# One step of a hybrid attention layer: keys and queries stored in DRAM with both parts of a row side by side, and output weights scaled while they are rounded

## The chip, the cores and the metric

The kernel runs on one NeuronCore of a Trainium2 chip. The metric is the device time of one launch in microseconds (us), the median of several runs; lower is better. TensorE (PE) does the matmuls and transposes, VectorE (DVE), ScalarE (ACT) and GpSimd (POOL) the rest, and nearly all DMAs are issued by SyncE (SP), in order, on one queue.

## The reference

One layer is run for a prompt of 2048 tokens and for a sample of 64 tokens that has a cache of 512 earlier ones. All is float32; the model width is 1024.

```python
h = rmsnorm(x, g_pre)
fq, fk, fv, ff, fg, dq, dk, dv, dg = split(h @ w_in)    # eight groups of 512 columns, ff of 8
# fox: 8 heads of 64; cum = cumulative sum of log_sigmoid(ff + b_f)
s = fq . fk / 8 + cum[query] - cum[key];  causal;       fox_o  = softmax(s) @ fv
# diff: 4 heads with two query/key halves of 64 and values of 128
s1, s2 = q1 . k1 / 8 + bias, q2 . k2 / 8 + bias;        # T5 bias, mask by chunks of 64
diff_o = rmsnorm((softmax(s1) - lam * softmax(s2)) @ dv, subln_g) * 0.8
out = concat(fox_o * silu(fg), diff_o * silu(dg)) @ w_out
y = x + rmsnorm(out, g_post)                            # also returned: k, v, log-forget rows
```

## The kernel before

**Two parts of a value.** Matmuls run on float32r operands. A value x is kept as h, its rounding to float32r, and l, the exact rest; a product takes three matmuls (h by h, h by l, l by h). Rounding is a copy on ScalarE that writes h, and a subtraction on VectorE or GpSimd that writes l.

**Stages.** The prompt is cut into four blocks of 512 tokens; the sample joins block 0. `Proj.block` multiplies a block with the eight groups of 512 weight columns. Keys (`k_out`), values (`v_out`), gates (`g_out`) and queries (`qgroup`) go to scratch tensors in DRAM, from which `Attn` loads them. The attention of a block goes on beside the projection of the next; the output projection (`Out`) goes on beside the attention of the last block. There are eight units, four pairs of fox heads and four diff heads; a unit has two "heads" `hd` in the scores (two fox heads, or the two halves of a diff head).

**The order.** Every piece of work is a function with a place on one line that is measured in TensorE time; the pieces are emitted in the order of their places, and a planner sets semaphores and the order of each engine's queue. The loads of the attention run ahead in rings: `Ring` issues the next load when a slot is freed. `caps = (4, 4, 6, 2, 2)` are the slots for keys, values, queries, biases and gates.

**Keys.** A score needs q.k with h and l parts. A head's keys are an operand of 128 rows: the 64 rows of the h part and the 64 rows of the l part, so that one matmul of 128 rows by the queries (h over l) gives hh + ll, and a second by the queries (l over h) gives the mixed products. In DRAM there is a tensor `KS[b]` per block of [2 heads, 8 units, 128 rows, 512 keys]. `k_out` turns a tile of 128 tokens over on TensorE, splits it into h and l in a slot `khl`, and stores it with two DMAs, one per head (L968). `want_k` loads an operand tile of up to 1024 keys with a DMA per block (L194).

**Queries.** `QD[b]` is [2, 8, 128, 512] (576 for block 0, with the sample). `qgroup` scales a piece (512 tokens; in block 0 two pieces of 288) into `qf`, rounds it into one half of a slot `qhl` (L1015), writes the rest into the other half (L1017), and stores it with one DMA per head (L1019). The slots `qhl`, `khl` and `vhl` share a tag with two buffers, so a slot must be stored before the next but one piece is rounded. `want_q` makes two tiles for 256 queries of a head: the (h over l) one with one DMA (L267), and the (l over h) one with two DMAs of 64 rows each (L270).

**Running sums.** `CUM[b]` holds [8, 512] per block; `want_cum` loads up to 1024 of them, repeated over all partitions, with a DMA per block (L285).

**Output weights.** `Out.weights` loads w_out in 16 pieces of 128 by 512 for k = 0 to 7, rounds each on ScalarE (L1200) and lets GpSimd compute the rest (L1201). For the diff heads, k = 4 to 7, ScalarE scales the piece in place first (L1199). Its place is the end of the last projection. The output projection uses k in the order 4, 5, 6, 7, 0, 1, 2, 3 (L1274 to L1276; L1269 and L1270 for the sample).

Of the kernel before, what the change touches and what calls it, by code (L numbers as in the profile page):

```python
# [9 lines left out]
F32 = mybir.dt.float32  # L10
# [7 lines left out]
P = 128  # L18
# [15 lines left out]
# T5 bucket of rel = key - query over the runs of rel in which it is constant  # L34
# (NUM_BUCKETS = 32, MAX_DISTANCE = 128, bidirectional); every rel below -90 is bucket 15.
# [10 lines left out]
class Ring:  # L46
    """Loads that run ahead of their use, as many as there are free slots."""
# [43 lines left out]
def hybrid_step(ctx: ExitStack, tc: tile.TileContext, ins, outs):  # L91
# [43 lines left out]
    QD = [dr.tile([2, 8, P, BLK + (DEC if b == 0 else 0)], F32, name=f"QD{b}") for b in range(NBLK)]  # L135
# [4 lines left out]
    CUM = [dr.tile([8, BLK], F32, name=f"CUM{b}") for b in range(NBLK)]  # L140
# [5 lines left out]
    def rsqrt_newton(pool, v, out, rows, n, tag, eng=None):  # L146
        """out = 1/sqrt(v): exp(-ln(v)/2) and one Newton step."""
# [11 lines left out]
    # ------------------------------------------------------------------ attention  # L159
    class Attn:  # L160
        """Attention of one range of query tiles, over every unit (two fox heads or one diff head)."""
# [9 lines left out]
        def asked(self):  # L171
            """A thunk that queues the loads asked for since the last call."""
# [9 lines left out]
        # ---- loads  # L182
        @staticmethod
        def key_edges(nk):
            """The keys of every tile of them: two blocks, or one at the front."""
            at = list(range(nk % (2 * BLK), nk, 2 * BLK))
            return list(zip([0] + at, at + [nk])) if at[:1] != [0] else list(zip(at, at[1:] + [nk]))

        def want_k(self, got, u, hd, nk):
            def load(k0, k1):  # L190
                def go():
                    t = self.p["k"].tile([P, 2 * BLK], F32R, name="kg", tag="k")
                    for c in range(k0, k1, BLK):
                        nc.sync.dma_start(out=r32(t[:, c - k0:c - k0 + BLK]), in_=KS[c // BLK][hd, u])  # L194
# [5 lines left out]
        def want_kc(self, got, u):  # L200
            """The sample's keys of a unit: both heads' operands, the cached ones and the new ones."""
# [13 lines left out]
            def second():  # L215
# [5 lines left out]
                # the order of the parts doesn't matter  # L221
# [38 lines left out]
        def want_q(self, got, u, hd, col, w):  # L260
            def load(s):
                def go():
                    t = self.p["q"].tile([P, 256], F32R, name="qg", tag="q")
                    src = QD[0] if col >= SEQ else QD[col // BLK]
                    c0 = BLK if col >= SEQ else col % BLK
                    if s == 0:
                        nc.sync.dma_start(out=r32(t[:, :w]), in_=src[hd, u, :, c0:c0 + w])  # L267
                    else:
                        for a in (0, 64):
                            nc.sync.dma_start(out=r32(t[a:a + 64, :w]), in_=src[hd, u, 64 - a:P - a, c0:c0 + w])  # L270
                    got.append(t)
                return go
            for s in (0, 1):
                self.want(self.Q, load(s))

        def want_cum(self, got, h, nk, sample):
            def load(c0, w):
                def go():
# [3 lines left out]
                    else:  # L282
                        for a in range(c0, c0 + w, BLK):
                            ww = min(BLK, c0 + w - a)
                            nc.sync.dma_start(out=t[:, a - c0:a - c0 + ww],  # L285
                                              in_=bcast_row(CUM[a // BLK][h, 0:ww], ww))
# [5 lines left out]
        def want_strip(self, got, h, nk, sample):  # L292
            """The bias of the last columns up to the diagonal; before them it is that of bucket 15."""
# [46 lines left out]
            # chunks of at most a bank, none narrow where that can be avoided  # L340
# [46 lines left out]
        def store_mix(self, mix, u, pair, w):  # L387
            """mix: f32 [128 mix columns, w tokens], in SBUF."""
            nc.sync.dma_start(out=(MN if pair is None else MS[pair])[u], in_=mix[:, :w])

        # ---- sub-jobs: (A thunks, B thunks, thunks of the step after)
        def fox(self, u, hd, pair, ctxu, first, last, sample=False):
            """One head, one pair of query tiles (or the sample's tile)."""
# [7 lines left out]
            for j, t in enumerate(tiles):  # L401
# [14 lines left out]
                if j == len(tiles) - 1:  # L416
                    def endA():
                        self.Q.free(); self.Q.free()
# [1084 lines left out]
```

## Time and profile before

| What | Value |
|---|---|
| Runs | 1841.08, 1832.17 and 1841.0 us; median 1841.0 |
| Span of the profiled execution, first to last instruction | 1837.8 us; the page gives no time around it |
| Busy: PE, DVE, ACT, POOL | 1736.8, 1189.6, 1128.9, 768.2 us |
| Mean granted TensorE clock | 0.982 |
| DMA | 308170 packets, 361.38 MB, 197 GB/s over the span |

Lines of the profile name a line of the kernel (L351), the engine, the operation, and the tiles as output<-inputs with shapes. A group shows its count, busy time, the mean in ns of one, then the engine's idle time just before its instructions and what ended that idle time. A row of waits reads: who waited, for whom, us in total, number of times, the longest. A row of windows holds the stretch, its length, busy time and number of instructions of PE, PE's weight loads, DVE, ACT and POOL, then the granted clock (1.00 is full), the busy share of the DMA engines, and GB/s. A row of a source line shows a queue's instruction with count, the shortest, median and longest time of its issue in ns, and the first and last start. A row of DMA issues ends with KB per DMA and the median us from issue to landing.

### The profile page before, as it was taken

Reading aid. Unit: us, or ns where it says so; the run is one execution under the profiler, and the core shown is the slowest. Engines: PE = TensorE matmul, PEld = TensorE weight load, DVE = VectorE, ACT = ScalarE, POOL = GpSimd, SP = SyncE. Lnnn points to the kernel's source line nnn. Section 1 sums busy time; section 2 is a strip of 40 time slices with the busy share of each in tenths; the row PEclk is TensorE's granted clock in tenths of the full one; section 3 lists DMA queues with packets and bytes.
Section 4 is the critical chain, followed back from the end, with each engine's and each line's share of the span. In section 5 each row is a group of like instructions: output and inputs, shape, how many; then the busy total and the mean of one; then the engine's idle time right before and its main releaser. Section 6 shows DMA issues by size and latency. Waiting matters only on the chain. (4 is left out here: it accounts for less than half of the span.)

```text
span 1837.8 us, 31858 instructions
## 1 busy us (share of the span) xinstructions
PE 1736.8 (95%) x9828; PEld 1467.4 (80%) x9828; DVE 1189.6 (65%) x3274; ACT 1128.9 (61%) x2518; POOL 768.2 (42%) x1083
## 2 busy tenths in 40 slices
PE   7888999999999999989999999999989999999998
PEld 5676888777877778878888888888878878887887
DVE  5422555556668576656776678878867876666764
ACT  4533656465767666665666657667776666556663
POOL 2204235345354453343323225555795663322331
PEclk9998999999999999999999999999989999999999
DMA  7787579789868766867777667667665464455433
GB/s 203 240 193 193 162 217 273 205 245 233 218 209 246 213 196 195 233 170 230 219 229 224 177 181 216 195 195 224 199 219 166 145 189 156 153 181 156 145 115 108
DMA packets 308170, 361.38 MB, mean 197 GB/s; under 512 B 41808, under 2 KB 202732, under 8 KB 308000
## 3 DMA queue, kind: packets, MB, share of 16 engines
q1 hardware_dynamic: 306384, 356.93, 66.9%
q0 software_dynamic: 672, 2.38, 0.4%
q8 instruction: 79, 1.29, 0.3%
q14 instruction: 91, 0.75, 0.1%
q10 hardware_dynamic: 944, 0.03, 0.0%
HBM read 263.89 MB, written 97.70 MB: 197 GB/s over the span
## 5 line engine op out<-in xcount | busy, mean ns | idle before, releaser
L372 ACT ACTIVATE prob<-prob,mn 128x1024 f32<-128x1024 f32 (+8 forms) x400 | 356.1, 892 | 180.7 <-DVE mn L359 179.5
L351 PE MATMUL S<-kg,qg 128*128 128x512 f32 (+4 forms) x1344 | 375.8, 373 | 20.5 <-DVE mn L359 10.0
L497 DVE TENSOR_TENSOR ptl<-pt,pth 128x512 fp32r<-128x512 f32 (+3 forms) x456 | 284.4, 636 | 94.8 <-ACT pth L496 92.3
L868 PE MATMUL acc<-wh,xx 128*128 128x512 f32 x752 | 303.4, 408 | 18.9 <-ACT wh L776 14.9
L869 PE MATMUL acc<-wl,xx 128*128 128x512 f32 x752 | 300.6, 401 | 8.5 <-DVE wl L777 8.5
L870 PE MATMUL acc<-wh,xx 128*128 128x512 f32 x752 | 300.6, 400 | 0.1
L496 ACT CAST pth<-pt 128x512 fp32r<-128x512 f32 (+3 forms) x456 | 237.6, 545 | 81.9 <-PE pt L490 65.4
L351 PEld LDWEIGHTS S<-kg,qg 128*128 128x128 f32 (+1 forms) x1344 | 226.6, 188 | 62.0 <-DVE mn L359 18.8
L490 PE MATMUL pt<-ident,prob 128*128 128x128 f32 (+2 forms) x1692 | 257.6, 274 | 4.7 <-ACT pts L637 2.2
L490 PEld LDWEIGHTS pt<-ident,prob 128*128 128x128 f32 (+2 forms) x1692 | 200.2, 142 | 26.6 <-ACT pts L637 3.3
L777 POOL TENSOR_TENSOR wl<-wraw,wh 128x512 fp32r<-128x512 f32 x126 | 167.4, 1345 | 121.2 <-ACT wh L776 91.0
L408 POOL TENSOR_TENSOR dg<-bias,cmask 128x128 f32<-128x128 f32 (+1 forms) x136 | 66.1, 486 | 281.8 <-DVE mn L359 188.4
L868 PEld LDWEIGHTS acc<-wh,xx 128*128 128x128 f32 x752 | 144.2, 193 | 49.7 <-ACT wh L776 17.2
L869 PEld LDWEIGHTS acc<-wl,xx 128*128 128x128 f32 x752 | 144.6, 192 | 37.3 <-DVE wl L777 11.5
L521 PE MATMUL av<-pth,vg 128*128 128x256 f32 (+1 forms) x576 | 158.3, 294 | 9.4 <-DVE oT L537 4.7
L870 PEld LDWEIGHTS acc<-wh,xx 128*128 128x128 f32 x752 | 144.0, 191 | 28.4 <-DVE xx L745 0.6
L521 PE MATMUL av<-ptl,vg 128*64 128x256 f32 (+1 forms) x576 | 140.3, 283 | 3.9 <-DVE ptl L497 3.6
L776 ACT CAST wh<-wraw 128x512 fp32r<-128x512 f32 x168 | 100.5, 618 | 69.1 <-DMA wraw<-in_w_in 59.9
L359 DVE CUSTOM_DVE_ANT_0 prob<-S,bias,mn 128x512 f32<-128x512 f32 (+4 forms) x200 | 115.3, 577 | 28.8 <-DMA bias<-CUM 14.5
L521 PE MATMUL avd<-pth,vg 128*128 128x256 f32 (+1 forms) x576 | 131.6, 288 | 2.3 <-ACT pth L496 2.3
L521 PEld LDWEIGHTS av<-pth,vg 128*128 128x128 f32 x576 | 110.0, 191 | 21.5 <-issue 7.7
L453 POOL TENSOR_SCALAR gate<-gate,rr 128x64 f32<-128x64 f32 (+1 forms) x136 | 61.5, 463 | 140.2 <-DMA gate<-GS 57.9
(257 smaller groups left out, 3611.8 us busy)
## 6 DMA issues: line engine op xcount, KB each, us to landing
wraw<-in_w_in SPq DMA_DIRECT2D x168, 256.0 KB, 4.8
vg<-VS SPq DMA_DIRECT2D x80, 512.0 KB, 4.1
kg<-KS SPq DMA_DIRECT2D x160, 256.0 KB, 4.1
bias<-CUM SPq DMA_DIRECT2D x80, 256.0 KB, 5.6
wst<-in_w_in SPq DMA_DIRECT2D x64, 256.0 KB, 5.6
out<-ef SPq DMA_DIRECT2D x64, 256.0 KB, 3.3
VS<-vhl SPq DMA_DIRECT2D x32, 512.0 KB, 4.6
KS<-khl SPq DMA_DIRECT2D x64, 256.0 KB, 4.7
```

The costliest lines, as they stand in the source:

```text
L351: nc.tensor.matmul(S[:rows, :c1 - c0], q()[s][:, qc:qc + rows], kg()[ki][:, c0 - k0:c1 - k0], start=(s == 0), stop=(s == 1))
L359: nc.vector.tensor_tensor_reduce(out=pr[:rows, a - p0:b - p0], in0=S[:rows, a - c0:b - c0], in1=ap()[:rows, a - b0:b - b0], scale=1.0, sca ...
L372: nc.scalar.activation(out=pr, in_=pr, func=AF.Exp, scale=-1.0, bias=st["m"][:rows, i - 1:i], accum_out=st["s"][:rows, h:h + 1])
L490: nc.tensor.transpose(pt[:rk, off:off + rows], self.key_tile(sts[j], rows, kt, rk), ident[:rows, :rows])
L496: nc.scalar.copy(h[:rk, :off], pt[:rk, :off])
L497: nc.vector.tensor_tensor(out=l[:rk, :off], in0=pt[:rk, :off], in1=r32(h[:rk, :off]), op=ALU.subtract)
L521: nc.tensor.matmul(st["av"][:vs.stop - vs.start, j0 * rows:W], ctxu["v"][kt // 4][:rk, kt % 4, vs], g["p"][part][:rk, o:o + w], start=(kt ...
L776: nc.scalar.copy(h, raw[:, :BLK])
L777: (nc.vector if many or k % 4 == 3 else nc.gpsimd).tensor_tensor(out=l, in0=raw[:, :BLK], in1=r32(h), op=ALU.subtract)
L868: nc.tensor.matmul(a, x[0][:, c0:c0 + rows], wh, start=s, stop=False)
L869: nc.tensor.matmul(a, x[0][:, c0:c0 + rows], wl, start=False, stop=False)
L870: nc.tensor.matmul(a, x[1][:, c0:c0 + rows], wh, start=False, stop=e)
```

## The change

Keys of the whole prompt lie in one tensor `KS` of [128 rows, 8 units, 2 parts, 2048]: rows 0 to 63 are head 0, 64 to 127 head 1, and the h and l parts of a row are next to each other in the third dimension. A tile of keys is stored with one DMA. An operand tile of up to 1024 keys is loaded with one DMA of 64 rows by 2 parts; its rows are then h, l, h, l in turn instead of all h and then all l. A row of queries is stored per pair of tiles as h, l, h (3 x 256), so that one load with overlapping reads makes both operands, (h, l) rows and (l, h) rows, side by side in one tile of 512 columns; this takes a second store of the h part. The ring of queries has 3 slots of twice the width instead of 6. Block 0's queries are cut in pieces of 256 and 256 + 64 tokens instead of 288 and 288, and the sample's 64 go to a tensor `QN` of their own. The running sums lie in one tensor. The output weights are taken in the order 4 to 7, 0 to 3; for the diff heads ScalarE scales and rounds in one instruction, and the rest is computed on VectorE with the scale in the same instruction. All comments are dropped as well.

```diff
-    KS = [dr.tile([2, 8, P, BLK], F32, name=f"KS{b}") for b in range(NBLK)]
+    KS = dr.tile([P, 8, 2, SEQ], F32, name="KS")
-    QD = [dr.tile([2, 8, P, BLK + (DEC if b == 0 else 0)], F32, name=f"QD{b}") for b in range(NBLK)]
+    QD = [dr.tile([8, P, 3 * BLK], F32, name=f"QD{b}") for b in range(NBLK)]
+    QN = dr.tile([8, P, 3 * DEC], F32, name="QN")
-    CUM = [dr.tile([8, BLK], F32, name=f"CUM{b}") for b in range(NBLK)]
+    CUM = dr.tile([8, SEQ], F32, name="CUM")
...
-                    for c in range(k0, k1, BLK):
-                        nc.sync.dma_start(out=r32(t[:, c - k0:c - k0 + BLK]), in_=KS[c // BLK][hd, u])
+                    nc.sync.dma_start(out=r32(t[:, :k1 - k0]), in_=KS[hd * 64:hd * 64 + 64, u, :, k0:k1])
...
+            def go():
+                t = self.p["q"].tile([P, 512], F32R, name="qg", tag="q")
+                rows = slice(hd * 64, hd * 64 + 64)
+                if col >= SEQ:
+                    for o in (0, 64):
+                        nc.sync.dma_start(out=r32(t[o:o + 64, :2 * w]), in_=QN[u, rows, o:o + 2 * w])
+                else:
+                    c0 = 3 * (col % BLK)
+                    a = QD[col // BLK][u, rows, c0:c0 + 2 * w]
+                    nc.sync.dma_start(out=r32(t[:, :2 * w]),
+                                      in_=bass.AP(a.tensor, a.offset, [a.ap[0], [w, 2], a.ap[1]]))
+                got.extend((t[:, :w], t[:, w:2 * w]))
+            self.want(self.Q, go)
...
-                        for a in range(c0, c0 + w, BLK):
-                            ww = min(BLK, c0 + w - a)
-                            nc.sync.dma_start(out=t[:, a - c0:a - c0 + ww],
-                                              in_=bcast_row(CUM[a // BLK][h, 0:ww], ww))
+                        nc.sync.dma_start(out=t[:, :w], in_=bcast_row(CUM[h, c0:c0 + w], w))
...
-            for i, a in enumerate((0, 64)):
-                nc.sync.dma_start(out=sc[i, u0:u0 + 4, :, r0:r0 + rows].rearrange("u (s r) t -> r (u s) t", s=2),
-                                  in_=r32(hl[a:a + 64, :, :rows]))
+            if t == 16:
+                ...
+            else:
+                nc.sync.dma_start(out=KS[:, u0:u0 + 4, :, t * P:(t + 1) * P].rearrange("r u s t -> r (u s) t"),
+                                  in_=r32(hl[:, :, :rows]))
...
+            pieces = [[(0, 2, 256)]] if nt <= BLK else [[(0, 1, 256)], [(256, 1, 256), (BLK, 1, DEC)]]
...
+                        for s0, n, m in segs:
+                            o = s0 - t0
+                            v = hl[:, 2 * o:2 * (o + n * m)].rearrange("p (a v t) -> p a v t", a=n, v=2)
+                            d = (QN[u0 + c] if s0 == BLK else
+                                 QD[b][u0 + c, :, 3 * s0:3 * (s0 + n * m)]).rearrange("p (a z) -> p a z", a=n)
+                            fs = f[:, o:o + n * m].rearrange("p (a t) -> p a t", a=n)
+                            nc.scalar.copy(v[:, :, 0], fs)
+                            nc.vector.tensor_tensor(out=v[:, :, 1], in0=fs, in1=r32(v[:, :, 0]), op=ALU.subtract)
+                            nc.sync.dma_start(out=d[:, :, 2 * m:], in_=r32(v[:, :, 0]))
+                            nc.sync.dma_start(out=d[:, :, :2 * m],
+                                              in_=r32(v).rearrange("p a v t -> p a (v t)"))
...
-            for k in range(KC):
+            for k in (4, 5, 6, 7, 0, 1, 2, 3):
...
                         if k >= 4:
-                            nc.scalar.activation(out=raw[:, :BLK], in_=raw[:, :BLK], func=AF.Copy, scale=subl)
-                        nc.scalar.copy(h[:, :BLK], raw[:, :BLK])
-                        nc.gpsimd.tensor_tensor(out=l[:, :BLK], in0=raw[:, :BLK], in1=r32(h[:, :BLK]),
-                                                op=ALU.subtract)
+                            nc.scalar.activation(out=h[:, :BLK], in_=raw[:, :BLK], func=AF.Copy, scale=subl)
+                            nc.vector.scalar_tensor_tensor(out=l[:, :BLK], in0=raw[:, :BLK], scalar=subl,
+                                                           in1=r32(h[:, :BLK]), op0=ALU.mult, op1=ALU.subtract)
+                        else:
+                            nc.scalar.copy(h[:, :BLK], raw[:, :BLK])
+                            nc.gpsimd.tensor_tensor(out=l[:, :BLK], in0=raw[:, :BLK], in1=r32(h[:, :BLK]),
+                                                    op=ALU.subtract)
...
-    caps = (4, 4, 6, 2, 2)
+    caps = (4, 4, 3, 2, 2)
```

More of the change, by code (lines that the diff above doesn't have):

```diff
@@ L260, in want_q @@
         def want_q(self, got, u, hd, col, w):
[L261 to L274, printed above, removed]
+            def go():
[11 more added lines that the diff above has]
+            self.want(self.Q, go)
         def want_cum(self, got, h, nk, sample):
@@ L417, in endA @@
                     def endA():
-                        self.Q.free(); self.Q.free()
+                        self.Q.free()
                         if last:
@@ L604, in endA @@
             def endA():
-                for _ in range(4):
+                for _ in range(2):
                     self.Q.free()
@@ L966, in k_out @@
             nc.vector.tensor_tensor(out=l, in0=x, in1=r32(h), op=ALU.subtract)
-            for i, a in enumerate((0, 64)):
-                nc.sync.dma_start(out=sc[i, u0:u0 + 4, :, r0:r0 + rows].rearrange("u (s r) t -> r (u s) t", s=2),
-                                  in_=r32(hl[a:a + 64, :, :rows]))
+            if t == 16:
+                for i, a in enumerate((0, 64)):
+                    nc.sync.dma_start(out=KN[i, u0:u0 + 4].rearrange("u (s r) t -> r (u s) t", s=2),
+                                      in_=r32(hl[a:a + 64, :, :rows]))
+            else:
+                nc.sync.dma_start(out=KS[:, u0:u0 + 4, :, t * P:(t + 1) * P].rearrange("r u s t -> r (u s) t"),
+                                  in_=r32(hl[:, :, :rows]))
         def g_out(self, g, t, f, rows):
@@ L986, in qgroup @@
             u0 = 0 if g == "fq" else 4
-            nb = 1 if nt <= BLK else 2
-            N = nt // nb
+            pieces = [[(0, 2, 256)]] if nt <= BLK else [[(0, 1, 256)], [(256, 1, 256), (BLK, 1, DEC)]]
             th = []
@@ L991, in qgroup, with step @@
                 e = {}
-                for i in range(nb):
-                    def step(k, c=c, i=i, e=e):
+                for i, segs in enumerate(pieces):
+                    t0 = segs[0][0]
+                    N = sum(n * m for _, n, m in segs)
+                    def step(k, c=c, i=i, e=e, t0=t0, N=N):
                         def go():
@@ L999, in go @@
                             o = e[i][:, :N]
-                            cs, xs_ = slice(c * P, (c + 1) * P), slice(i * N, (i + 1) * N)
+                            cs, xs_ = slice(c * P, (c + 1) * P), slice(t0, t0 + N)
                             nc.tensor.matmul(o, wh[:, cs], xh[:, xs_], start=(k == 0), stop=False)
@@ L1003, in go @@
                             nc.tensor.matmul(o, wl[:, cs], xh[:, xs_], start=False, stop=(k == KC - 1))
-                            if c == 3 and i == nb - 1 and freew:
+                            if c == 3 and i == len(pieces) - 1 and freew:
                                 self.W.free()
@@ L1007, in qgroup, with evac @@
                     th += [(3 * N / 2400.0, step(k)) for k in range(KC)]
-                    def evac(c=c, i=i, e=e):
+                    def evac(c=c, i=i, e=e, segs=segs, t0=t0, N=N):
                         f = self.p["e"].tile([P, BLK], F32, name="qf", tag="ef")
                         hl = self.p["e"].tile([P, 2 * BLK], F32R, name="qhl", tag="er", bufs=2)
-                        h, l = hl[:, :N], hl[:, N:2 * N]
-                        nc.vector.tensor_tensor(out=f[:, :N], in0=e[i][:, :N], in1=st["rbc"][:, i * N:(i + 1) * N],
+                        nc.vector.tensor_tensor(out=f[:, :N], in0=e[i][:, :N], in1=st["rbc"][:, t0:t0 + N],
                                                 op=ALU.mult)
-                        nc.scalar.copy(h[:, :N], f[:, :N])
-                        nc.vector.tensor_tensor(out=l[:, :N], in0=f[:, :N], in1=r32(h[:, :N]), op=ALU.subtract)
-                        for j, a in enumerate((0, 64)):
-                            nc.sync.dma_start(out=QD[b][j, u0 + c, :, i * N:(i + 1) * N].rearrange("(s r) t -> r s t", s=2),
-                                              in_=r32(hl[a:a + 64, :2 * N]).rearrange("r (s t) -> r s t", s=2))
+                        for s0, n, m in segs:
[9 more added lines that the diff above has]
+                                              in_=r32(v).rearrange("p a v t -> p a (v t)"))
                     th.append((0.5, evac))
@@ L1152, in sums @@
                 nc.vector.tensor_copy(cumlast, cum[:, BLK - 1:BLK])
-                nc.sync.dma_start(out=CUM[b], in_=cum)
+                nc.sync.dma_start(out=CUM[:, b * BLK:(b + 1) * BLK], in_=cum)
             def sample():
@@ L1181, in weights @@
         def weights(self):
-            self.w = []
+            self.w = {}
             th = []
-            for k in range(KC):
+            for k in (4, 5, 6, 7, 0, 1, 2, 3):
                 def go(k=k):
```

4 lines of the change are left out of this document (1 added, 3 removed).

## The prediction

> **What bounds the kernel now.** I read the page's first part, then TensorE's waits, then windows of the stages that the change touches, and last the issues of SyncE's queue.
>
> ```profile
> span 1837.8 us, 31858 instructions
> PE 1736.8 (95%) x9828; PEld 1467.4 (80%) x9828; DVE 1189.6 (65%) x3274; ACT 1128.9 (61%) x2518; POOL 768.2 (42%) x1083
> ```
> ```profile
> PE acc L868 <- ACT wh L776: 14.9, 7, 5.9
> PE S L351 <- DVE mn L359: 10.0, 13, 2.7
> PE acc L869 <- DVE wl L777: 8.5, 2, 5.0
> PE S L351 <- DMA qg<-QD: 5.8, 6, 2.5
> ```
> ```profile
> 300.00:900.00 600.00, 567.54 (x3156) 467.99 (x3155) 384.10 (x1103) 379.67 (x900) 258.37 (x403) 0.98 0.77 217
> 900.00:1300.00 400.00, 392.30 (x2308) 337.30 (x2307) 301.15 (x848) 269.33 (x591) 168.92 (x216) 1.00 0.70 203
> ```
>
> TensorE is busy for 1736.8 of 1837.8 us, so everything that is not TensorE can give at most 101 us, and that is split over many small waits: the longest group is 14.9 us. The change removes no matmul, so its gain can only come out of these waits and out of the time at a lower granted clock. From 300 to 900 us TensorE idles 600 - 567.5 = 32.5 us; from 900 to 1300 us it idles only 7.7 us. The two stretches differ in what their rows show beside it: the DMA engines are 0.77 against 0.70 busy.
>
> **The loads.** The rows of the queue, and the issues with their time to landing:
>
> ```profile
> L267 SPq DMA_DIRECT2D qg<-QD x144: 319/386/1775, 143.2 to 1735.8; - x144
> L270 SPq DMA_DIRECT2D qg<-QD x288: 444/522/1989, 144.9 to 1737.4; - x144
> L194 SPq DMA_DIRECT2D kg<-KS x160: 319/422/1775, 137.5 to 1717.4; - x160
> L285 SPq DMA_DIRECT2D bias<-CUM x80: 319/426/2224, 81.8 to 1750.4; - x80
> L968 SPq DMA_DIRECT2D KS<-khl x64: 580/627/1722, 109.6 to 1291.4; - x64
> L1019 SPq DMA_DIRECT2D QD<-qhl x80: 574/610/1852, 139.2 to 1217.1; - x80
> ...
> qg<-QD SPq DMA_DIRECT2D x128, 128.0 KB, 3.1
> qg<-QD SPq DMA_DIRECT2D x256, 64.0 KB, 4.0
> kg<-KS SPq DMA_DIRECT2D x160, 256.0 KB, 4.1
> KS<-khl SPq DMA_DIRECT2D x64, 256.0 KB, 4.7
> ```
>
> Queries: each of 128 operands (a pair of tiles, a head) needs one issue of 0.386 us and two of 0.522 us, 1.43 us. One load replaces them. Its source has three dimensions; its issue costs between 0.386 us (L267, two dimensions) and 0.610 us (L1019, three). I take 0.5, between them, since its other side is a plain tile as in L267. That frees 128 x 0.93 = 119 us of SyncE; the sample's 16 operands go from three issues to two, 8 us. Keys: 16 x (1+2+3+4) = 160 loads become 16 x (1+1+2+2) = 96, 64 x 0.422 = 27 us. The running sums go from 80 to 48 the same way, 32 x 0.426 = 14 us. Key stores: 64 become 32, 20 us. Query stores: a piece of 512 tokens still has two; the first block's 16 pieces have 32 stores now and 8 x 2 + 8 x 4 = 48 afterwards, 16 x 0.61 = 10 us more. In sum 178 us of issue time leave SyncE.
>
> SyncE's time is not on TensorE's path by itself. What is on it is the lateness of an operand, and in the waits of TensorE no key load appears, only queries: 5.8 us in six waits. The last of three query loads lands about 0.39 + 0.52 + 0.1 (gaps) + 3.9 = 4.9 us after the first issue begins; one load of 256 KB, by the nearest row of that size (the keys'), lands after 4.1 us. Six waits shortened by 0.8 us each, none below nothing, are 4 of the 5.8 us. What comes late next is the keys' load, which is issued just before the queries and has 0.8 us less in hand; no wait shows it.
>
> The clock goes with the waits:
>
> ```profile
> 355.00:360.00 5.00, 2.15 (x9) 1.33 (x8) 0.03 (x1) 0.00 (x0) 0.00 (x0) 1.00 0.82 215
> 360.00:365.00 5.00, 4.73 (x24) 3.88 (x23) 2.26 (x7) 3.92 (x10) 0.00 (x0) 0.66 0.51 163
> 510.00:515.00 5.00, 3.67 (x15) 2.97 (x14) 1.79 (x8) 0.95 (x3) 2.16 (x7) 0.66 0.36 113
> ```
>
> Behind two of the query waits the granted clock is 0.66 over 5 us, which loses 5 x 0.34 = 1.7 us each time. With 4 of 5.8 us of wait gone I take the same share, 2.3 of 3.4 us. The Trainium skill (TensorE: Matmul & The Clock Gate, Part 1) puts the drop to half clock behind an idle window of about 3.4 us; by that rule no wait here (the longest is 2.5 us) would cost any clock, and the loads' term would be 2.3 us smaller. The trace disagrees: TensorE was busy for 2.15 of the 5 us ahead of the first drop and the clock fell all the same.
>
> Loads queued behind the queries come sooner too, of which the projection's weights matter:
>
> ```profile
> PE acc L868 <- ACT wh L776: 2.5, 3, 1.4
> PE acc L868 <- ACT xx L744: 0.9, 1, 0.9
> ```
>
> These are TensorE's waits between 300 and 900 us that a late weight or token load ends through ScalarE, 3.4 us; I take 1. Loads: 4 + 2.3 + 1 = 7.3 us, with ends at nothing (hidden anyway) and at 5.8 + 3.4 + 3.4 = 12.6 us.
>
> **The output weights.**
>
> ```profile
> L1199 ACT ACTIVATE wor<-wor,subl 128x512 f32<-128x512 f32 x8 | 5.4, 713 | 0.2 <-DMA wor<-in_w_out 0.2
> L1200 ACT CAST woh<-wor 128x512 fp32r<-128x512 f32 x8 | 5.0, 623 | 0.0
> L1201 POOL TENSOR_TENSOR wox<-wor,wox 128x512 fp32r<-128x512 f32 x8 | 10.4, 1296 | 0.0
> L744 ACT ACTIVATE xx<-xraw,gcol 128x512 fp32r<-128x512 f32 x24 | 16.2, 721 | 5.7 <-DMA xraw<-in_xT 3.7 <-PE pt L490 1.8 <-PE acc L870 0.2
> L745 DVE SCALAR_TENSOR_TENSOR xx<-xraw,gcol,xx 128x512 fp32r<-128x512 f32 x24 | 18.0, 773 | 2.8 <-ACT xx L744 2.8
> L777 DVE TENSOR_TENSOR wl<-wraw,wh 128x512 fp32r<-128x512 f32 x42 | 41.2, 980 | 15.7 <-ACT wh L776 15.7
> ...
> 1340.00:1360.00 20.00, 18.33 (x110) 16.01 (x109) 14.98 (x35) 18.33 (x40) 19.71 (x21) 0.94 0.73 236
> 1360.00:1380.00 20.00, 16.47 (x74) 13.04 (x73) 12.06 (x33) 14.70 (x30) 17.73 (x16) 0.72 0.61 184
> ...
> PE S L351 <- DVE mn L359: 2.3, 2, 2.1
> PE avd L521 <- DVE ptl L497: 1.7, 2, 1.0
> PE pt L490 <- ACT pts L637: 0.7, 1, 0.7
> PE ptg L551 <- POOL gate L644: 0.5, 1, 0.5
> ```
>
> The last four rows are TensorE's waits from 1350 to 1380 us, 5.2 us; the clock costs 20 x 0.06 + 20 x 0.28 = 6.8 us more: 12.0 us are lost where the weights are rounded, with GpSimd busy 19.7 and 17.7 of 20 us and ScalarE 18.3 and 14.7. For each of eight pieces the scaling (0.713 us) and the rounding copy (0.623 us) become one scaled rounding, 0.721 us by L744: ScalarE gives 8 x 0.615 = 4.9 us. GpSimd gives 8 x 1.30 = 10.4 us. VectorE takes 8 x 0.773 = 6.2 us, and waits for ScalarE in front of each as L777 does there (15.7 / 42 = 0.37 us), 3 us; queued behind it are the minima that free the scores' banks, and TensorE waits for those. VectorE is busy 27 of these 40 us, so 9 us fit. The two engines that were full become free and the free one becomes fuller: I take half of the 12.0 us, 6. The ends are all 12.0 gained, and 3 lost if VectorE's waits reach TensorE whole. That the diff heads' weights are rounded first follows the order in which the output projection uses them; it adds nothing that I could price apart.
>
> **The query stores.** A piece now stores 256 KB twice; afterwards 512 KB and 256 KB, because the first part of a row is kept twice. Over 24 pieces that is 24 x 256 KB = 6.3 MB; in the first block 4 stores of 144 KB become 864 KB for each of eight column groups, 2.4 MB more: 8.7 MB in a stretch that moves 217 GB/s at a DMA share of 0.77. I cost the bytes at nothing in the blocks behind the first, where other loads run ahead in their slots. In the first block there is no such cover:
>
> ```profile
> ACT qhl L1015 <- DMA QD<-qhl: 12.5, 5, 3.8
> ACT qhl L1015 <- DMA KS<-khl: 10.0, 2, 9.1
> ...
> PE acc L868 <- ACT wh L776: 4.4, 1, 4.4
> PE acc L869 <- DVE wl L777: 3.5, 1, 3.5
> ...
> 150.00:160.00 10.00, 5.11 (x12) 3.60 (x13) 5.81 (x17) 5.64 (x12) 10.00 (x26) 0.53 0.61 132
> ```
>
> ScalarE stands at the rounding of a query piece until one of two slots has been stored, and behind it in its queue are the weights' copies for which TensorE waits 4.4 and 3.5 us between 130 and 160 us, with the clock at 0.53 afterwards. Four of the eight pieces of that group get two more stores of 0.61 us, 4.9 us of SyncE; the eight small copies and differences for the sample's 64 columns are shorter than the 0.62 us of a copy of 512 and lie in the waits. Against it SyncE loses there four key stores (4 x 0.63 = 2.5 us) and two of every three query loads that it issues there. I take 2.5 us lost; the ends are 2 gained (the key stores that held ScalarE for 9.1 us land sooner) and 9 lost (twice the 4.9 less 0.8, if bytes and issues both reach TensorE).
>
> **The sum.** -7.3 - 6 + 2.5 = -10.8 us: 1837.8 becomes 1827 for the span. The runs shown are 1841.1, 1832.2 and 1841.0; their median is 3.2 us over the span, so I predict 1841.0 - 10.8 = 1830 us. The ends of the three terms are -12.6 - 12.0 - 2 = -26.6 and 0 + 3 + 9 = +12. Under about 0.5%, 9.2 us, a measurement of this kernel can't tell from no change (the three runs lie 8.9 us apart), so 1831.8 and 1850.2 are the bounds.
>
> **Rivals.** First, the queue matters beyond the waits that carry its name: with 178 us of issues gone, the middle stretch idles like the later one, 600 x 7.7 / 400 = 11.6 instead of 32.5 us, 21 us. With the clock's 2.3, the weights' 6 and the stores' 2.5 that is -27, 1814 us. For it: the denser stretch is the idler one. Against it: only 5.8 + 3.4 us of its waits lead back to a load.
>
> Second, the loads are hidden anyway: the query waits are moved, not removed (the next load in the in-order queue is late), and VectorE gives back what ScalarE and GpSimd gain. Only the stores' 2.5 us remain: 1843.5 us. For it: 95% busy, and most waits of TensorE are on ScalarE and VectorE.
>
> Third, on the other side: the larger query stores hold their slots longer in every block. There are 40 pieces; if each delays TensorE by x, the time is 1841 - 13.3 + 40x, and it passes 1850.2 at x = 0.56 us. At one store's issue, 0.61 us, it is 1852 us. For it: the two slots already hold ScalarE for 12.5 us in the first block. Against it: all five of those waits lie there.
>
> Fourth, the new key tensor has 128 KB from row to row. If that halves the rate, a key store lands after 9.4 instead of 4.7 us, and the first block's ScalarE wait of 9.1 us grows by 4.7 us: 1835 us. The Trainium skill (DMA: Bandwidth & Descriptors, Latency and other measured facts) lists slower copies where row pitches are large powers of two, with 207 GB/s at 512 KiB against 214; at that loss it would cost next to nothing, and no run here shows it.
>
> **Chances.** The forecast 0.42, of which 0.26 faster, 0.14 within, 0.02 slower; the first rival 0.20, faster; the second 0.17, of which 0.14 within and 0.03 slower; the third 0.15, slower; the fourth 0.06, of which 0.05 within and 0.01 slower. Faster 0.46, within 0.33, slower 0.21. The forecast's own range is 1814 to 1853; for 8 in 10 over all cases I give 1806 to 1853.
>
> **What would show it.** SyncE's query issues fall from 432 to 160, with the load landing near 4.1 us; TensorE's waits for queries fall below 2 us; between 1340 and 1380 us the clock stays above 0.9 and GpSimd is no longer full; ScalarE's waits for query stores in the first block grow from 12.5 us. The prediction is wrong if the query waits stay at 5.8 us with fewer issues, if VectorE's minima hold TensorE longer where the weights are rounded, or if the stores' waits show in the later blocks.

## The result and the profile after

The changed kernel takes 1789.8 us (median; 1787.5 to 1793.0) beside 1839.4 us (1832.2 to 1841.1) for the kernel before: a ratio of 0.9753, 95% interval 0.9722 to 0.9783. A second comparison, on another chip, gave 0.976 (0.9734 to 0.9786). The forecast of 1830 us had the sign right and the size wrong: the span fell by 1837.8 - 1789.3 = 48.5 us where 10.8 were worked out, and the range ended at 1806.

The head of the page of the changed kernel:

```profile
span 1789.3 us, 31315 instructions
PE 1714.0 (96%) x9828; PEld 1459.2 (82%) x9828; DVE 1193.4 (67%) x3290; ACT 1126.0 (63%) x2518; POOL 762.8 (43%) x1075
```

TensorE's idle time fell from 101.0 to 75.3 us, 26 of the 48.5. The other 22.8 came out of its busy time, with the same 9828 matmuls: that is the first thing that the forecast had hardly counted. TensorE's waits, the same view as before:

```profile
PE acc L867 <- ACT wh L775: 14.3, 4, 5.9
PE S L350 <- DVE mn L358: 9.9, 14, 1.9
...
PE acc L868 <- DVE wl L776: 5.2, 1, 5.2
...
PE S L350 <- DMA qg<-QN: 0.6, 1, 0.6
```

The waits for `qg<-QD` (5.8 us) are gone, as forecast; of the rest, the largest two groups are as long as they were. The named waits explain little. The windows explain more, here the two stretches of before and the two around the output weights:

```profile
300.00:900.00 600.00, 583.87 (x3340) 487.99 (x3339) 402.10 (x1171) 397.83 (x941) 273.14 (x418) 1.00 0.77 234
900.00:1300.00 400.00, 396.11 (x2317) 342.12 (x2316) 305.23 (x843) 274.28 (x602) 183.13 (x222) 1.00 0.68 213
1300.00:1340.00 40.00, 35.65 (x202) 30.17 (x201) 37.59 (x81) 30.56 (x65) 37.00 (x37) 0.96 0.74 235
1340.00:1380.00 40.00, 38.68 (x228) 33.43 (x228) 31.30 (x79) 25.52 (x56) 23.14 (x24) 1.00 0.50 153
```

From 300 to 900 us TensorE now does 3340 instead of 3156 instructions, 5.8% more, and 5.8% of 600 us is 35 us. Half of that is idle time (32.5 us became 16.1). The other half is time per instruction: 567.5 / 3156 = 0.1798 us became 583.9 / 3340 = 0.1748, and 3340 of that difference are 17 us. Before, the clock's records have TensorE at half clock for 20.5 us of this stretch, after for none; that is worth up to 10 us. The rest is in stalls inside the busy time and in what kinds of instruction fall into the stretch, and was not taken apart.

A second measure cuts the time in two whatever the order within: the last matmul of the projection (tile `acc`). Its row for the kernel before, and after:

```profile
L870 PE MATMUL acc<-wh,xx x752: 387/389/729, 14.0 to 1345.5; 128*128 128x512 f32 x188
```
```profile
L869 PE MATMUL acc<-wh,xx x752: 387/389/774, 14.2 to 1305.7; 128*128 128x512 f32 x188
```

39.8 us of the 48.5 are there by the end of the projection; the stage behind it went from 492.3 to 483.6 us.

The issues of SyncE's queue after, in two views:

```profile
L273 SPq DMA_DIRECT2D qg<-QD x128: 517/566/2065, 147.9 to 1684.0; - x128
```
```profile
qg<-QD SPq DMA_DIRECT2D x128, 256.0 KB, 4.2
kg<-KS SPq DMA_DIRECT2D x64, 512.0 KB, 4.9
KS<-khl SPq DMA_DIRECT2D x32, 512.0 KB, 5.4
```

One query load takes 0.566 us to issue (0.5 was taken) and lands after 4.2 us (4.1). Over the launch SyncE issues 1299 DMAs instead of 1683. Summed over its instructions in the trace, it is busy for 61.7% of the stretch from 300 to 900 us before and for 47.3% after; this figure is called the share of the queue below.

### The profile page after: what moved, and what is told of

It is laid out like the page before. It is cut to its first block, busy times and chain, and to the rows that moved or that the text cites. A ratio compares the mean times of both kernels' runs of the same rounds, so it can differ in the third digit from the quotient of the medians.

```text
span 1789.3 us, 31315 instructions
## 1 busy us (share of the span) xinstructions
PE 1714.0 (96%) x9828; PEld 1459.2 (82%) x9828; DVE 1193.4 (67%) x3290; ACT 1126.0 (63%) x2518; POOL 762.8 (43%) x1075
## 5 line engine op out<-in xcount | busy, mean ns | idle before, releaser
L350 PE MATMUL S<-kg,qg 128*128 128x512 f32 (+4 forms) x1344 | 369.8, 371 | 12.5 <-DVE mn L358 9.9
L489 PE MATMUL pt<-ident,prob 128*128 128x128 f32 (+2 forms) x1692 | 253.4, 272 | 2.5 <-DVE mix L553 1.0
L776 POOL TENSOR_TENSOR wl<-wraw,wh 128x512 fp32r<-128x512 f32 x126 | 173.1, 1392 | 85.7 <-ACT wh L775 84.7
L867 PEld LDWEIGHTS acc<-wh,xx 128*128 128x128 f32 x752 | 143.8, 192 | 48.0 <-ACT wh L775 16.1
```

The costliest lines, as they stand in the source:

```text
L350: nc.tensor.matmul(S[:rows, :c1 - c0], q()[s][:, qc:qc + rows], kg()[ki][:, c0 - k0:c1 - k0], start=(s == 0), stop=(s == 1))
L489: nc.tensor.transpose(pt[:rk, off:off + rows], self.key_tile(sts[j], rows, kt, rk), ident[:rows, :rows])
L776: (nc.vector if many or k % 4 == 3 else nc.gpsimd).tensor_tensor(out=l, in0=raw[:, :BLK], in1=r32(h), op=ALU.subtract)
L867: nc.tensor.matmul(a, x[0][:, c0:c0 + rows], wh, start=s, stop=False)
```

## The experiments

Three explanations stood against each other. **Q**: room on SyncE's in-order queue is what counts; with it loads and stores of every kind come sooner. **P**: the gain is a matter of the planner, which sets the order of each engine's queue by its own model of time; in the first runs that meant that the reordering is needed for the gain, in the last ones that most of it is the luck of one order. A third (T, or the wider loads) held that the transfers themselves make the difference; and W, in the last runs, that the output weights are worth something once the loads no longer hold.

**With the reordering switched off**, each engine takes its instructions in the order in which the kernel's text emits them.

```diff
-    with tile.TileContext(nc, schedule_with_timeline_sim=True) as tc:
+    with tile.TileContext(nc, schedule_with_timeline_sim=False) as tc:
```

Before, in that order: 

> The kernel before, with the planner's reordering by its own model of time switched off, so that the queues follow the program nearly as it is written. It is the base for the next two; no theory says what it takes itself. It is read against e2 and e3. If the change gains because SyncE's queue is relieved (theory Q), e2 is some 45 us (2.5%) below this. If it gains because the planner, given other loads, puts TensorE's work in another order (theory P: 3933 of 9825 TensorE instructions are in common order between the two kernels as measured, 9038 with the reordering off), e2 is within 10 us of this.

After, in that order: 

> The changed kernel with the reordering switched off. Theory Q: 45 us below e1. Theory P: within 10 us of e1. The rival that the weights carry it: 6 to 12 us below e1.

After, in that order, with 384 tiny stores in SyncE's queue, ahead of the loads and stores that had been merged:

```diff
+    PAD = dr.tile([512, 64, 4], F32, name="PAD")
+    def pad(n):
+        for _ in range(n):
+            nc.sync.dma_start(out=PAD[next(pads)], in_=ident[:64, :4])
...
+                    pad((k1 - k0) // BLK - 1)      # ahead of a load of keys; 2 ahead of one of queries,
+                                                   # w // BLK - 1 of sums, 1 ahead of a store of keys
```

> e2 with 384 tiny stores of 16 bytes on 64 rows put on SyncE's queue where the change took issues out: two ahead of each query load, one ahead of each merged key load, sums load and key store. They move almost no data (0.4 MB), and TensorE's order stays that of e2. If SyncE's issue time is what counts (Q), it loses what e2 gained over e1, to within 10 us. If the number and size of the loads' packets or the layout counts, it stays within 10 us of e2. Theory P says nothing of it but that it is near both.

Measured against the kernel before (1829.8 us on that chip): 1946.6 us, ratio 1.0633 (1.0595 to 1.0671); 1947.7 us, 1.0643 (1.0604 to 1.0683); 1988.7 us, 1.0868 (1.0832 to 1.0904). The rows of 300 to 900 us, of e1, of e2 and of e3:

```profile
300.00:900.00 600.00, 554.43 (x2971) 441.06 (x2970) 351.81 (x1033) 369.78 (x863) 246.32 (x394) 0.97 0.73 207
```
```profile
300.00:900.00 600.00, 551.50 (x2993) 440.60 (x2992) 358.15 (x1042) 371.93 (x868) 247.01 (x395) 0.97 0.73 215
```
```profile
300.00:900.00 600.00, 537.92 (x2840) 428.64 (x2839) 343.59 (x996) 359.10 (x846) 242.38 (x391) 0.95 0.73 208
```

In the written order the change gives nothing, though the share of the queue falls from 59.1% to 42.4% just as it does in the planned order: the time saved became SyncE's waiting. Q's number (45 us) failed here and P's (within 10 us) held. So a shorter queue is not enough by itself. That it is worth something where the order of the engines lets the earlier operands be used is the reading that fits, not one that was tested. The tiny stores cost 41 us over e2 even so, although e1, with nearly as full a queue (59.1% against 62.9%), loses nothing. The traces show one difference: the idle time of ScalarE, VectorE and GpSimd that the landing of a DMA ended (their rows of waits that name a DMA, added up from 300 to 900 us) is 103 us in e1 and in e2, and 147 us in e3.

**One part alone.** The loads without the output weights, and the output weights without the loads (each is the other part of the diff undone):

> The changed kernel with the output weights' part undone (order 0 to 7, scaling in place, rest on GpSimd). My prediction's terms: 6 us above the changed kernel, 1796. If the weights carry more than predicted: up to 12 us above, 1802. If they are hidden: 1790.

> The kernel before with the output weights' part alone (order 4 to 7 then 0 to 3, scaled while rounded, rest on VectorE). In e4 the loads alone gave 18 us of the change's 45, and after the last projection they gave 8 us back. If the weights' gain is their own, 12 to 27 us below the kernel before; if it is mostly what e4 lost in its last stage by another order, 5 to 9 us below; as predicted, 6.

Measured: 1811.8 us, ratio 0.9897 (0.9862 to 0.9933), and 1827.3 us, 0.9989 (0.9971 to 1.0007). The weights alone are worth nothing that can be told. The loads alone seemed to leave 27 us to the weights on top of them; two more orders of the same kernel (e16 and e18, below) take that back.

**The changed kernel with its queue filled again**: the 384 tiny stores, with the reordering on.

> The changed kernel with 384 tiny stores on SyncE's queue where the change took issues out, with the planner reordering as in the changed kernel. If SyncE's issue time is the cause (Q), 35 to 45 us over the changed kernel, level with the kernel before. If it is the shape and size of the loads, within 10 us of the changed kernel. If it is the planner's order (P), which sees these stores too, anything between, with TensorE's order changed.

Measured: 1873.2 us, ratio 1.0230 (1.0190 to 1.0271), some 88 us over the changed kernel, twice what Q gave, and slower than the one before. The tiny stores depend on nothing, and the planner issued them early, as the row of their line shows; the windows stand behind it:

```profile
L144 SPq DMA_DIRECT2D PAD<-ident x384: 445/594/2269, 36.2 to 705.5; - x192
```
```profile
300.00:900.00 600.00, 546.51 (x2948) 447.94 (x2947) 352.42 (x1034) 361.48 (x866) 252.46 (x399) 0.96 0.76 217
900.00:1300.00 400.00, 396.56 (x2364) 343.76 (x2363) 303.44 (x862) 267.41 (x580) 164.04 (x209) 1.00 0.69 217
```

The loss lies exactly where the tiny stores are. Three eighths through the projection it has grown to 43 us, six eighths through (980 us) to 83, and then it stays: from 900 to 1300 us the kernel runs as densely as the unpadded one. All merged loads are still merged, so this loss is not one of wide against narrow loads. Nor does the tiny stores' own traffic account for it: their 24576 packets of 16 bytes took 9 ns each in the trace, 13 us of each DMA engine's time over the whole launch, while SyncE was busy with its DMAs for 909 instead of 663 us. The share of the DMA engines (0.76 against 0.77) settles nothing here, since it is 0.74 to 0.78 in every run with the reordering on, whatever the GB/s. The queue is busy for 68.7% of 300 to 900 us.

**One kind of load taken apart again**, queries in three, then keys and sums by block:

```diff
-                    nc.sync.dma_start(out=r32(t[:, :2 * w]), in_=...)            # e7: three loads, as before
+                    nc.sync.dma_start(out=r32(t[:, :w]), in_=...)
+                    for o in (0, 1):
+                        nc.sync.dma_start(out=r32(t[64 * o:64 * o + 64, w:2 * w]), in_=...)
```
```diff
-                    nc.sync.dma_start(out=r32(t[:, :k1 - k0]), in_=KS[hd * 64:hd * 64 + 64, u, :, k0:k1])
+                    for c in range(k0, k1, BLK):                                 # e8; the sums likewise
+                        nc.sync.dma_start(out=r32(t[:, c - k0:c - k0 + BLK]), in_=KS[hd * 64:hd * 64 + 64, u, :, c:c + BLK])
```

> The changed kernel with each query operand loaded by three DMAs again (128 KB and twice 64 KB, rows h and l in turn), all else as changed. Q by count: the queries are 256 of the net 384 issues and 119 of 178 us, so 25 to 30 us over the changed kernel. My prediction: 4 to 6 us over. If the keys and sums carry it: under 3 us.

> The changed kernel with the keys' and sums' loads cut into one per block of 512 again, all else as changed (96 more issues, 41 us of SyncE). Q by count: 8 to 12 us over the changed kernel. My prediction: nothing. If the wider loads of keys and sums carry it: 20 us or more.

And all of them together, which brings 352 loads back under the new layouts:

> The changed kernel with all its merged loads taken apart again, queries in three, keys and sums per block: the 384 issues are back, the layouts in DRAM, the stores and the output weights stay as changed. Theory Q: the losses of e7 and e8 add up, 1788 + 31 + 15 = 1834, and SyncE's queue is about as full as in the kernel before (0.65 of the stretch from 300 to 600 us, where the changed kernel has 0.50). Theory P (luck of an order): anywhere between 1800 and 1840, not below 1795.

Measured: e7 1816.0 us, ratio 0.9918 (0.9887 to 0.9950); e8 1801.5 us, 0.9842 (0.9811 to 0.9873); e14 1825.3 us, 0.9976 (0.9953 to 1.0000). Against 0.976 that is 0.016, 0.008 and 0.022, or 29, 15 and 40 us: the parts add up to a little more than the whole, and with all loads apart nearly the whole gain is gone. Q gave 25 to 30 us for e7, 8 to 12 for e8 and 1834 us for e14: right, somewhat low, and 9 us high. The windows of e7, of e8 and of e14:

```profile
300.00:900.00 600.00, 573.41 (x3180) 475.23 (x3178) 389.16 (x1109) 380.51 (x905) 264.40 (x405) 0.98 0.77 227
```
```profile
300.00:900.00 600.00, 580.55 (x3297) 484.65 (x3296) 399.00 (x1161) 395.13 (x932) 269.61 (x415) 0.99 0.77 233
```
```profile
300.00:900.00 600.00, 570.31 (x3196) 472.99 (x3195) 390.29 (x1119) 381.98 (x907) 264.95 (x407) 0.99 0.77 225
```

Read beside the share of the queue in the same 600 us, TensorE's instructions fall in step, with one small inversion: 47.3% and 3340 (after), 50.4% and 3297 (e8), 57.7% and 3180 (e7), 61.4% and 3196 (e14), 61.7% and 3156 (before), 68.7% and 2948 (e6). The other orders of the next part fall in line: 60.9% to 61.8% and 3168 to 3200 with the old loads, 46.7% to 48.6% and 3310 to 3344 with the new ones. In these orders the query loads are two thirds of the effect; the 15 us of e8 alone are less than a change of order can do (below).

These three runs do not tell issue time from transfer time for the queries. Added up over all packets, a DMA engine was busy for 1200 us after, 1202 in e8, 1229 in e7, 1232 in e14 and 1247 before, so taking the query loads apart also gave the DMA engines some 30 us more to do. That SyncE's time is what counts rests on e6 (1242 us there, of which the tiny stores' packets are 13; the other packets took longer for the same bytes).

**The luck of one order.** The lag of the attention behind the projection was changed by half a microsecond, which does no work but gives another order (3008 to 5295 of TensorE's 9825 instructions keep their place in the sequence).

```diff
-    LAG = 5
+    LAG = 5.5          # or 4.5
```

The changed kernel again, and nudged both ways: 

> The changed kernel, once more, beside the kernel before on this chip: both theories 0.972 to 0.979 of before, some 1785 us where before takes 1830. It is the common measure for the three runs beside it.

> The changed kernel with one number changed that does no work: the lag of the attention behind the projection is 5.5 instead of 5 us, which is enough for the planner to find another order (5295 of TensorE's 9825 instructions still stand in the same order). Theory P (a good deal of the 48 us is the luck of the order that the planner found): 10 us or more above the changed kernel, 1795 to 1825. Theory Q (fewer issues on the in-order queue of SyncE let the planner find a denser order, whichever one it finds): within 8 us of the changed kernel.

> The same with a lag of 4.5 us (4378 of 9825 instructions in the same order). Theory P: 10 us or more above the changed kernel, 1795 to 1825. Theory Q: within 8 us of it.

The kernel before, nudged: 

> The kernel before with a lag of 5.5 us (3008 of 9825 instructions in the same order, fewer than the change itself leaves in order). Theory P: the kernel before was an unlucky order, so this lands 10 to 30 us lower, 1800 to 1820. Theory Q: within 8 us of before, since nothing left SyncE's queue.

> The kernel before with a lag of 4.5 us: a third order of it (5131 of 9825 instructions in the same order). Theory Q with W (the loads are worth some 35 us up to the end of the projection, the output weights some 9 behind it): the projection's last matmuls at 1334 to 1346 us, 488 to 500 us from there to the end, 1830 to 1842 in all. Theory P (luck of an order): the projection's end anywhere from 1305 to 1346, and a total down to 1805.

The loads alone, nudged: 

> The loads alone, without the change of the output weights, and with the lag of the attention at 5.5 instead of 5 us. Theory P for the weights: e4's last stage was an unlucky order, so this lands at 1790 to 1803, beside the changed kernel with the same nudge (1803). Theory W (the weights' part is worth 27 us once the loads no longer hold): 1820 to 1832.

> The loads alone with a lag of 4.5 us: a third order of it. Q with W: the projection's last matmuls at 1300 to 1313 us, 490 to 500 us from there to the end, 1795 to 1812 in all. If the output weights' part were luck alone, the last stage would as soon take 480 to 488 us.

| Ratio to before (95%) | lag 5 | 5.5 | 4.5 | mean |
|---|---|---|---|---|
| before | 1 | 1.0052 (1.0031-1.0073) | 0.9996 (0.9974-1.0019) | 1.002 |
| loads alone | 0.9897 (0.9862-0.9933) | 0.9833 (0.9799-0.9866) | 0.9768 (0.9741-0.9795) | 0.983 |
| after | 0.9760 (0.9734-0.9786) | 0.9836 (0.9808-0.9865) | 0.9806 (0.9775-0.9838) | 0.980 |

| End of projection / stage behind it, us | lag 5 | 5.5 | 4.5 |
|---|---|---|---|
| before | 1345.5 / 492.3 | 1338.4 / 496.5 | 1333.6 / 487.1 |
| loads alone | 1304.3 / 500.2 | 1311.1 / 491.5 | 1299.7 / 485.1 |
| after | 1305.7 / 483.6 | 1312.3 / 488.7 | 1300.2 / 491.5 |

The nudges put the changed kernel 15.5 and 8.6 us higher and the kernel before 8.1 us higher and 3.3 lower. P's number holds for the first of these alone, and Q's is missed by less than 1 us for the two between. For the last, Q gave an end of the projection at 1334 to 1346 us, 488 to 500 us behind it and 1830 to 1842 us in all; all three came out just below (1333.6, 487.1, 1828.1), within what P allowed. Luck is there, and it is smaller than the difference between the rows of before and after.

A change of order that does no work moves a kernel by up to 1.3%, 24 us (the loads alone). Over three orders each, the loads are worth 1.8%, 34 us (19, 40 and 42 us lag by lag), and all of it is there at the end of the projection (means 1339.2 and 1305.0 us; no order of the one comes within 20 us of the other). The output weights on top are worth 0.3%, 6 us, less than the spread of either row, and the stage behind the projection, where they are used, overlaps: 487 to 497 before, 485 to 500 with the loads alone, 484 to 492 after. For e16 the explanation by luck gave 1790 to 1803 us and W 1820 to 1832; it took 1797.6. For e18 W's 490 us or more behind the projection (485.1) and 1795 us or more in all (1786.6) failed. What the change is worth without luck is about 40 us (44, 40 and 35 lag by lag); the changed kernel's own order is some 8 us better than the mean of its three.

**The tiny stores on GpSimd's queue** instead of SyncE's (`nc.gpsimd` for `nc.sync` in their one line), to tell the queue from the transfers: 

> The same 384 tiny stores as in e6 beside the changed kernel, but issued by GpSimd's queue instead of SyncE's. Theory Q (the room on SyncE's in-order queue is what counts): most of the 88 us goes, at most 25 us over the changed kernel, 1788 to 1813; what is left is GpSimd's own time for issuing. Theory T (the tiny transfers themselves, 64 packets of 16 bytes each, cost): still 1850 or more.

Measured: 1910.4 us, ratio 1.0440 (1.0407 to 1.0472). Q's number failed, but the test did not separate the two. The planner moved all 384 into the first 379 us, where GpSimd and TensorE's start suffered; the row of the line, two windows and two of TensorE's waits up to 160 us:

```profile
L144 POOL DMA_DIRECT2D PAD<-ident x384: 521/521/785, 1.7 to 378.7; - x192
```
```profile
0.00:150.00 150.00, 79.59 (x325) 60.32 (x325) 37.60 (x80) 40.64 (x74) 102.30 (x185) 0.82 0.58 142
900.00:1300.00 400.00, 396.50 (x2366) 341.66 (x2365) 297.31 (x856) 264.85 (x576) 160.71 (x215) 1.00 0.71 223
```
```profile
PE acc L877 <- ACT xx L753: 29.8, 3, 24.3
PE acc L877 <- ACT ef L887: 20.8, 1, 20.8
```

A DMA that GpSimd issues holds that engine for 0.52 us, and for more when it waits for earlier ones (47.2 us in 39 waits here). Two eighths through the projection 83 us are lost already.

**Still fewer issues on SyncE's queue**: the stores of values and gates issued by GpSimd, in whose queue they stand behind the instruction that makes their data.

```diff
-            nc.sync.dma_start(out=sc[r0:r0 + rows, u0:u0 + 4, :], in_=...)       # values; the gates' store likewise
+            nc.gpsimd.dma_start(out=sc[r0:r0 + rows, u0:u0 + 4, :], in_=...)
```

> The changed kernel with the stores of values and gates issued by GpSimd, which makes their data last, instead of SyncE: 68 issues and the 60 us that SyncE stands in its queue for GpSimd's results between 150 and 900 us are gone. Theory Q: 5 to 15 us faster than the changed kernel, 1773 to 1783. Against it: SyncE's queue is half empty already, so nothing, or a loss of up to 15 us by another order and by GpSimd's own issue time.

Measured: 1815.9 us, ratio 0.9920 (0.9890 to 0.9950), 29 us slower than the changed kernel, where Q expected a gain of 5 to 15. Its middle stretch is as it was:

```profile
300.00:900.00 600.00, 583.20 (x3316) 484.99 (x3315) 408.27 (x1168) 396.98 (x936) 280.35 (x443) 1.00 0.75 233
```

The share of the queue falls only to 46.2%, and six eighths through the projection the kernel stands where the changed one does (897.0 and 896.2 us); 7 us are lost at the end of the projection and 18.5 behind it (502.1 us), within or near what an order alone does there. So a little more room on a queue with room gave nothing; as the stores also take GpSimd's time, why the kernel became slower stays open. The Trainium skill (DMA: Bandwidth & Descriptors, Issuing engines are not separate DMA queues) says that issuing from several engines saves only the sequencer's time, usually small beside the DMA; the trace agrees for one DMA (0.566 us against 4.2 to landing). Here that saving brought nothing, while on the crowded queue of before 384 fewer issues came with 34 us.

## Why the prediction was right and wrong

**What bounds the kernel** was right: no matmul was removed, and all of the gain is TensorE's idle time and its time per instruction. But the ceiling of 101 us counted idle time alone, and the lower clock, named beside it, was priced behind a few waits only; 22.8 us came from busy time.

**The loads, -7.3 us forecast, -12.6 at most, is the term that failed**: e4, e16 and e18 measure -34 as a mean of three orders, and none less than 19. The working counted 178 us of issues off SyncE (the trace shows 872 - 663 = 209 us of its own time) and then wrote that "what is on it is the lateness of an operand", to be read from the six waits that carry the queries' name. That step is wrong. The six waits did go (5.8 to 0.6 us), but they are a third of the idle time that went between 300 and 900 us (16.4 us), and of the five drops of the clock there only two lay behind a query wait of more than 1 us. The longest drop, 6.8 us at half clock from 818.1 us, lay behind a wait for VectorE. These are waits of before from 800 to 820 us:

```profile
PE av L521 <- DVE oT L537: 4.7, 1, 4.7
ACT xn L1037 <- DMA xn<-in_xp: 3.9, 1, 3.9
DVE prob L359 <- DMA bias<-CS: 3.8, 1, 3.8
...
POOL gate L453 <- DMA gate<-GS: 3.5, 1, 3.5
```

ScalarE, VectorE and GpSimd all stand for some time between 806 and 811 us for loads that SyncE issued from 803.2 to 807.0 us, behind keys, queries and weights; from 813.6 us TensorE stands for VectorE. So what was missed, as far as the traces show it, is that loads of every kind stand in one in-order queue, and that late ones stop the other engines too: in TensorE's waits they carry other names. How one wait led to the next was not followed further.

The tally of idle time that a DMA ended on ScalarE, VectorE and GpSimd, from 300 to 900 us, goes that way: 158, 153 and 158 us in the three orders of before, 133 to 145 in the six with the new loads, 188 in e6. It does not sort every run (e14 has 147, e7 160, e5 177). One row of SyncE's own waits, for a free slot of the projection's weights, looks like the same thing, before and after:

```profile
SPq L773 <- POOL wl L777: 8.2, 8, 3.6
```
```profile
SPq L772 <- POOL wl L776: 27.5, 25, 3.5
```

After, SyncE stands ready for the next weights 25 times instead of 8. But this row is no measure of the gain: it reads 23.9 us, 22 times, in the slower e12, and 17.3 and 43.8 us in e1 and e2, which take the same time. How much of the 34 us comes from operands that land sooner, and how much from the order that the planner finds when it has fewer issues to place, no run separates; e1 and e2 show that without the reordering nothing comes of it, e3 that in a fixed order a fuller queue can cost 41 us.

The first rival had the place right, a middle stretch nearly as dense as the later one, but priced idle time alone: 21 us, where 16.4 went. Clock and time per instruction gave as much again.

**The second rival, loads hidden anyway**, holds in the written order (e1 and e2) and not in the planned ones.

**The output weights, -6 us**: in these two orders the stage behaves about as worked out. ScalarE scales and rounds in one instruction and VectorE makes the rest, in the rows of `wor`:

```profile
L1207 ACT ACTIVATE woh<-wor,subl x4: 717/717/722, 1300.0 to 1307.4; 128x512 fp32r<-128x512 f32 x4
...
L1208 DVE SCALAR_TENSOR_TENSOR wol<-wor,subl,woh x4: 739/748/2859, 1302.2 to 1310.2; 128x512 fp32r<-128x512 f32 x4
```

0.717 and 0.748 us were taken as 0.721 and 0.773, and 40 - 35.65 + 1.6 for the clock = 6.0 us are lost from 1300 to 1340 us where 12.0 were lost. But GpSimd is full all the same (37.0 of 40 us), against the forecast, and VectorE is now full beside it (37.6). Over three orders the part cannot be told from nothing (25, -1 and -7 us lag by lag; that their mean of 6 meets the forecast is luck), and alone it gave nothing (e5).

**The query stores, +2.5 us**, had the wrong sign if any. ScalarE's waits for slots in the first 300 us of the changed kernel:

```profile
ACT qhl L1024 <- DMA KS<-khl: 8.2, 1, 8.2
...
ACT qhl L1024 <- DMA QN<-qhl: 7.6, 2, 4.8
...
ACT qhl L1024 <- DMA QD<-qhl: 3.4, 2, 3.1
```

11.0 us for query stores stand against 12.5, and 8.2 for key stores against 10.0. A quarter of the projection is done at 229.4, 229.9 and 228.2 us in the three orders after, and at 233.9, 229.8 and 231.4 before: if anything a gain. The third rival fell: behind 300 us ScalarE never waits for a query store. So did the fourth: a key store of twice the bytes lands after 5.4 us where the halved rate would have given 9.4.

**The clock.** TensorE's time at half clock fell from 69.4 to 39.8 us in the records of the two profiles, and every drop between 160 and 1215 us is gone. In both profiles every drop follows 3.41 us (the shortest record) in which TensorE was busy for anything from 0 to 2.1 us, so not always idle. The rule of the Trainium skill weighed in the prediction (TensorE: Matmul & The Clock Gate, Part 1), that a window of about 3.4 us must be idle, leaves the drops behind waits of 2.5 us and less unexplained.

## What to carry to other kernels

Where one engine issues nearly all DMAs in order, read how full that engine is, stage by stage, and not only the waits that carry a DMA's name: here the fall from some 60% of its time to 47% came with 34 us, most of which stood under other engines' names or in no wait at all, and one point less (e15) brought nothing. Price such a change from the difference in density between a stretch with a crowded queue and one without, counting time per instruction and clock as well as idle time; here half of the gain in that stretch was there. And where a planner sets the order, run a nudge that does no work before crediting anything below its spread (here up to 24 us) to a part of a change.

## What the hardware showed that was not expected

- 384 stores of 1 KB on SyncE's queue, 0.594 us of issue each, cost 88 us, 0.23 us each, in a kernel whose TensorE is 96% busy, while their packets took 13 us of each DMA engine's time (e6).
- The same 384 fewer issues came with 34 us in the planned orders and with nothing in the written one (e1, e2).
- A DMA on GpSimd's queue held that engine for 0.52 us, and 39 of 384 had it wait for earlier ones first, 47.2 us in all (e13).
- TensorE's clock fell to half behind 3.41 us in which it had been busy for as much as 2.1 us (before, at 418.8 us).
